# A SwiGLU stage rewritten as one list of block products, with its loads and operand preparation issued further ahead

## The chip, the cores and the metric

One core of a Trainium2 chip runs the whole program. The metric is device time in microseconds of one execution, taken several times; lower is better. A core has five engines that each run their own instruction queue in order: TensorE (PE, matrix products into PSUM), VectorE (DVE, elementwise work), ScalarE (ACT, copies with rounding and activation functions), GpSimd (POOL, some elementwise work, and here mostly a queue that issues DMAs) and SyncE (SP, a queue that issues DMAs). DMA transfers run beside them. An instruction that waits holds up everything behind it on its own engine.

## The reference

A decoder layer on x of 1024 tokens by 1024 channels in float32. First a token mixer in three groups of channels, then the feed-forward part, which is what the change is about:

```python
    h = rms_norm(x, g_ffn[l])
    x = x + (jax.nn.silu(h @ w_gate[l]) * (h @ w_up[l])) @ w_down[l]
return rms_norm(x, g_final)
```

`w_gate` and `w_up` are 1024 x 2816, `w_down` is 2816 x 1024. Below, "gate/up" is the pair of products with `w_gate` and `w_up`, and "down" is the product with `w_down`.

## The kernel before

Every float32 product is made of three matmuls (`mm3`, lines 322 to 324) on a high and a low part of each operand. The high part is a rounded copy made on ACT, the low part is the difference, made on DVE.

**Gate/up.** The 2816 columns are taken in 11 blocks of 256. For each block there are two "halves", gate (j = 0) and up (j = 1): 22 objects of the class `Half`, numbered k = 2p + j. A half is a 2 x 2 block product done with seven block products instead of eight (the Strassen-Winograd scheme), numbered 1 to 7. One product is 4 x 3 = 12 matmuls of 128 x 128 by 128 x 512, so a half is 84 matmuls. The right operands are the activations (B11, B21, B22, T1 in the two big tiles `bb`, and T2, T3, T4 computed once by `t_ops`). The left operands come from the weights:

- `Half.load` reads two weight tiles r1 and r2 through SP (line 868) and lets a DMA from POOL add one part of r2 onto another (`add`, line 874: a DMA with accumulation).
- `prep("A1")` makes the high and low parts of r1 (`ha` on ACT at line 853, `la` on DVE at line 854) for products 1 and 2.
- `prep("S1")`, `prep("S2")`, `prep("S3")`, `prep("A22")`, `prep("S4")` each make the high part (`S.copy`, line 879, on ACT) and the low part (line 880, on DVE) of one operand. After S1 an accumulating DMA turns the same place of r2 into S2's sum; after S2 two more make the sums of S4 and S3. So S1, S2 and then S3 and S4 are a chain with a DMA between its links.
- Products 1 and 2 use A1, product 5 uses S1, 6 uses S2, 7 uses S3, 4 uses A22 and 3 uses S4.

The parts lie in a pool `s5` of N5 = 9 slots; A1 takes two and every other operand one, so a half takes seven. The weight tiles lie in `crx`, four slots, which is two halves. Evacuation from PSUM combines the seven products into the tiles c1 and c2: line 917 (ACT) after product 1, 918 after 2, 933 and 934 after 6, 938 and 939 after 7, 943 after 4, 948 after 3, all on DVE. Products 5 and 4 share the PSUM tag `px` with two buffers, and the buffer of product 5 is read last at line 939. Then c1 and c2 are scaled by the row norm (line 950) and, for gate, go through Silu on ACT (lines 952 and 953). When both halves of a block are done, `lefts` (lines 1030 to 1039) multiplies them, forms the seven left operands of down and stores them in DRAM (`actd`).

`Rights` (lines 757 to 784) does the same for the right operands of down: it loads `w_down` (line 768), makes four sums (lines 774 to 777) and stores them (`td`, line 782), all its DMAs through SP. `middle(k)` puts `Rights` and `lefts` of the half before into the middle of half k.

**The order.** The source gives each instruction a place; a planner (`schedule_with_timeline_sim=True`) then simulates the program and fills each engine's queue. It takes an instruction as soon as its simulated inputs and a free slot are there, and the place in the source is its priority. The function `behind(x, y)` only says that y comes after x in its queue. So the order in a queue can differ from the order in the source, and on the chip a queue keeps the planned order even where the real times differ. In the source of before, a half's operands are prepared between its own products: S1 after product 1, S2 after product 5, S3 after 6, A22 after 7, S4 after 4 (for the first block S2 and S4 before product 3). The weights of half k + 1 are loaded at the start of half k. The first two halves are interleaved (1, 2, 5, 3 of both, then the rest), and so are the last two: 1, 2, 5 of both, then 6, 7, 4, 3 alternately.

**Down.** 77 operand tiles (i, p): product i in the order 1, 2, 5, 6, 3, 7, 4, and block p from 0 to 10. A tile has a left half from `actd` (line 1174) and a right half from `w_down` or `td` (line 1175), 256 KB each, both through SP. The first 27 go to 27 slots laid over memory of gate/up: the first eight over the big tile of B11 and T1, the next eleven over the T operands, the last eight over the big tile of B21 and B22. Each tile is split into parts by ACT (line 1116) and DVE (line 1117) and used in 12 matmuls. The tile (1, 10), the last of product 1, needs `actd` of the last block, which `lefts` of the last two halves stores through POOL. After it come four loads of the residual x1 (1 MB each, line 1177) and of `g_final` (line 1178) through POOL; evacuation of product 1 adds onto the first of them.

Of the kernel before, what the change touches and what calls it, by code (L numbers as in the profile page):

```python
# [3 lines left out]

# [1 line left out]

# [5 lines left out]
F32 = mybir.dt.float32  # L12
# [6 lines left out]
P = 128  # L19
D = 1024  # L20
NT = 1024
KD = D // P
DFF = 2816
NF = DFF // P
# [8 lines left out]
N4, N5, NSB, NWO = (int(v) for v in '11,9,4,6'.split(","))  # L33
# [11 lines left out]
def trunk(ctx: ExitStack, tc: tile.TileContext, A, O):  # L45
    nc = tc.nc
    V, S, GP, PE, SY = nc.vector, nc.scalar, nc.gpsimd, nc.tensor, nc.sync
    mult, add, sub = ALU.mult, ALU.add, ALU.subtract

    def en(key, i=0, default="0"):  # L50
        v = ENG.get(key, default)
        return GP if v[i % len(v)] == "1" else V

    def behind(first, *later):

        for i in later:
            tc.add_manual_dep(i.ins, first.ins.name, mybir.DependencyInfo(mybir.DependencyClass.NoSync, mybir.DependencyReason.DATA), reason="order")
# [8 lines left out]
    x1d = dram.tile([P, 8, 2, 512], F32, name="x1d")  # L66
# [278 lines left out]
    for k in range(KD):  # L345
# [4 lines left out]
        w = load_w(k, 0, 384, V, V if k == 0 else S)  # L350
# [25 lines left out]
    with tc.high_priority():  # L376
# [32 lines left out]
    e = V  # L409
# [347 lines left out]
    class Rights:  # L757
# [3 lines left out]
            o.p, h = divmod(k, 2)  # L761
            o.c, o.n = slice(h * 256, h * 256 + 256), f"{o.p}{h}"

        def load(o, first):
            o.r = [tr.tile([P, 2, 256], F32, tag=f"t{q}", name=f"t{q}_{o.n}") for q in range(2)]
            o.x = tr.tile([P, 256], F32, tag="x", name=f"tx_{o.n}")
            for q, r in enumerate(o.r):
                i = SY.dma_start(r, wd[o.p, q].rearrange("r (q c) -> r q c", q=2)[:, :, o.c])
                if first is not None:
                    behind(first, i)  # L770

# [4 lines left out]
            V.tensor_tensor(r1[:, 1], r1[:, 1], r0[:, 1], add)  # L776
            V.tensor_tensor(r1[:, 0], r1[:, 0], r1[:, 1], add)

        def store(o, first):
            r0, r1 = o.r  # L780
            for d, t in ((td[o.p, 2, :, o.c], o.x), (td[o.p, 3, :, o.c], r0[:, 1]), (td[o.p, 0:2, :, o.c].rearrange("q r c -> r q c"), r1)):
                i = SY.dma_start(d, t)
                if first is not None:
                    behind(first, i)

# [72 lines left out]
    class Half:  # L858


        def __init__(o, p, j):
            o.p, o.j, o.P, o.w = p, j, {}, {}
            o.n = f"{p}{j}"

        def load(o):
# [40 lines left out]
                mm3(pz, h[:, ks], l[:, ks], rh, rl, kt == 0, kt == 3)  # L906
            o.P[i] = pz

        def first(o):
            a = slice(0, 512)  # L910
            if o is not g0:
                o.prep("A1")
            o.prod(1, "A11", "B11")
            o.prep("S1")
            o.prod(2, "A12", "B21")
            o.c1, o.c2 = (cc.tile([P, NT], F32, tag="c", name=f"c{q}{o.n}") for q in range(2))
            S.copy(o.c2[:, a], o.P[1])
            o.last1 = V.tensor_tensor(o.c1[:, a], o.P[2], o.c2[:, a], add)
            o.prod(5, "S1", "T1")
            o.prep("S2")  # L920
            if o.p == 0:
                o.prep("S4")
                o.prod(3, "S4", "B22")

        def second(o):
            for _ in o.steps():
                pass

        def steps(o):

            a, b = slice(0, 512), slice(512, 1024)
            o.prod(6, "S2", "T2")
            V.tensor_tensor(o.c2[:, a], o.c2[:, a], o.P[6], sub)
            V.tensor_tensor(o.c1[:, b], o.c2[:, a], o.P[5], sub)
            o.prep("S3")
            yield
            o.prod(7, "S3", "T3")
            V.tensor_tensor(o.c2[:, a], o.P[7], o.c2[:, a], add)
            V.tensor_tensor(o.c2[:, b], o.c2[:, a], o.P[5], sub)  # L939
            o.prep("A22")  # L940
            yield
            o.prod(4, "A22", "T4")
            V.tensor_tensor(o.c2[:, a], o.c2[:, a], o.P[4], sub)
            if o.p:
                o.prep("S4")
                yield
                o.prod(3, "S4", "B22")
            o.last = V.tensor_tensor(o.c1[:, b], o.P[3], o.c1[:, b], add)
            for q, c in enumerate((o.c1, o.c2)):
                en('rs', 2 * o.j + q, '0101').tensor_tensor(c, c, rsf, mult)  # L950
            if o.j == 0:
                S.activation(o.c1, o.c1, AF.Silu)
                S.activation(o.c2, o.c2, AF.Silu, scale=-1.0)

    g0 = Half(0, 0)
# [47 lines left out]
    def t_ops():  # L1003

        for name in ("T2", "T3", "T4"):
            for kt in range(4):
                t2 = t2r[kt // 2][:, kt % 2]
                e = t_slot(f"{name}_{kt}")
                tt_[name, kt] = e
                eg = en(name, kt).tensor_tensor  # L1010
                w = t2
                if name == "T3":
                    hi, lo = b_op("B11", kt)
                    if kt % 2 == 0:
                        wt = ct.tile([P, NT], F32, tag="t", name=f"w{name}{kt}")
                    w = wt[:, (kt % 2) * 512:(kt % 2) * 512 + 512]
                    eg(w, t2, hi, sub)
                    eg(w, w, lo, sub)
                elif name == "T4":
                    hi, lo = b_op("B21", kt)  # L1020
                    eg(w, hi, w, sub)
                    eg(w, w, lo, add)
                S.copy(e[:, 0], w)
                en(name, kt).tensor_tensor(e[:, 1], w, e[:, 0], sub)

    def lefts(p, g, u):

        a, b = slice(0, 512), slice(512, 1024)
        c1, c2, d1, d2 = g.c1, g.c2, u.c1, u.c2
        V.tensor_tensor(c1, c1, d1, mult)  # L1030
        V.tensor_tensor(c2, c2, d2, mult)
        V.tensor_tensor(d1[:, b], c1[:, a], c1[:, b], add)
        V.tensor_tensor(c1[:, b], c1[:, b], c2[:, b], add)
        V.tensor_tensor(d1[:, a], c1[:, a], c1[:, b], add)
        V.tensor_tensor(d2[:, a], d1[:, a], c2[:, a], add)
        e = GP if p == NF // 2 - 1 else S
        for q, t in ((0, c1), (2, c2), (4, d1)):
            e.dma_start(actd[p, q:q + 2].rearrange("q r c -> r q c"), t.rearrange("r (q c) -> r q c", q=2))
        e.dma_start(actd[p, 6], d2[:, a])

    NH = NF
    H = [g0] + [Half(*divmod(k, 2)) for k in range(1, NH)]
    R = [Rights(k) for k in range(NH)]

    def middle(k):

        ld = H[k + 1].ld if k + 1 < NH else None
        if k:
            R[k - 1].sums(H[k - 1].last)
            R[k - 1].store(ld)  # L1050
        R[k].load(ld)
        if k > 1 and k % 2 == 0:
            lefts(k // 2 - 1, H[k - 2], H[k - 1])

    H[0].first()
    H[1].load()
    H[1].first()
    t_ops()
    ffn_rms()
    R[0].load(H[1].ld)  # L1060
    H[0].second()
    H[2].load()
    R[0].sums(H[0].last)
    R[0].store(H[2].ld)
    R[1].load(H[2].ld)
    H[1].second()
    for k in range(2, NH - 2):
        H[k + 1].load()
        H[k].first()
        middle(k)  # L1070
        H[k].second()
    g, u = H[NH - 2:]
    u.load()
    g.first()
    middle(NH - 2)
    u.first()
    R[NH - 2].sums(g.last1)
    R[NH - 2].store(u.ld)
    R[NH - 1].load(u.ld)
    for _ in zip_longest(g.steps(), u.steps()):  # L1080
        pass
    lefts(NF // 2 - 1, g, u)
    R[NH - 1].sums(g.last)
    R[NH - 1].store(None)
    psA.close()
    scC.close()
    sc4.close()
# [83 lines left out]
    for m, (i, p) in enumerate(todo):  # L1171
        if m >= len(SLOTS):
            early[i, p] = dr.tile([P, NT], F32, tag=f"r{SLOTS[m % len(SLOTS)]}", name=f"d{i}_{p}")
        SY.dma_start(early[i, p][:, a], actd[p, LEFT[i]])
        SY.dma_start(early[i, p][:, b], right(i, p))
    for i, h in ((0, 0), (0, 1), (1, 1), (1, 0)):
        GP.dma_start(cs[i, h], x1d[:, 4 * i:4 * i + 4, h])
    GP.dma_start(gfin, A["g_final"])

    def acc(c, x, op=add):  # L1180
        V.tensor_tensor(c, c, x, op)  # L1181
# [112 lines left out]
```

## Time and profile before

| | us |
|---|---|
| median of 3 runs (1040.85 to 1049.59) | 1043.83 |
| the profiled execution | 1045.06 |
| its span, first to last instruction | 1043.0 |
| PE busy in the span | 944.2 |
| DVE busy | 759.4 |
| ACT busy | 353.3 |
| POOL busy | 213.8 |

The busy time of PE is close to the span, so what can be gained lies in the places where PE waits or runs at a reduced clock. The span has these stretches: the token mixer up to about 340 us, gate/up from there to about 800 us, down to the end. The clock row of the profile's second part tells at what share of full speed PE was allowed to run in each slice.

### The profile page before, as it was taken

To read this page: it belongs to the slowest core of one execution; us is meant where nothing else is said; L and a number is where in the kernel's file an instruction comes from. 1 tells how busy PE (TensorE), PEld (TensorE's weight loads), DVE (VectorE), ACT (ScalarE), POOL (GpSimd) and SP (SyncE) were. 2 spreads that over 40 slices of the span, in tenths; PEclk is the share of its full clock that TensorE was granted. 3 is DMA by queue.
4 is the path that set the end of the run, shared out by engine and by line. 5 is a ranking of instruction groups with operands and counts; after the bars stand their busy time and mean duration, and the time that the engine had idled before them with its cause. 6 is when DMAs were issued, how large, how long until landed. Compare 5 with 4: busy or idle time off the path is not lost. (4 is left out here: it accounts for less than half of the span.)

```text
span 1043.0 us, 12545 instructions
## 1 busy us (share of the span) xinstructions
PE 944.2 (91%) x4280; PEld 780.9 (75%) x4280; DVE 759.4 (73%) x1275; ACT 353.3 (34%) x535; POOL 213.8 (20%) x234
## 2 busy tenths in 40 slices
PE   9988898687997999989997998998997959999996
PEld 7887697466886778867886886876885848888884
DVE  7999988964558988758767687676878436456776
ACT  7524232234334433222321322213222234343543
POOL 0346444412201511111111111111110200000032
PEclk9999899898999899998998999999999979999999
DMA  7234424337123368776767776777765999763012
GB/s 261 81 96 82 120 71 111 100 73 201 51 101 101 61 170 245 204 180 192 197 188 189 191 201 175 210 203 178 202 178 179 397 387 386 243 195 108 1 41 121
DMA packets 102016, 173.84 MB, mean 167 GB/s; under 512 B 13009, under 2 KB 46561, under 8 KB 101953
## 3 DMA queue, kind: packets, MB, share of 16 engines
q1 hardware_dynamic: 69344, 113.21, 33.4%
q0 software_dynamic: 14416, 29.63, 14.7%
q10 hardware_dynamic: 18192, 30.21, 9.0%
q8 instruction: 33, 0.54, 0.2%
q14 instruction: 31, 0.25, 0.1%
HBM read 110.00 MB, written 41.68 MB: 145 GB/s over the span
## 5 line engine op out<-in xcount | busy, mean ns | idle before, releaser
L1117 DVE TENSOR_TENSOR ol<-d,oh 128x1024 fp32r<-128x1024 f32 x77 | 95.9, 1258 | 87.7 <-PE q L324 52.4
L880 DVE TENSOR_TENSOR S<-r,S 128x512 fp32r<-128x512 f32 x88 | 62.0, 706 | 106.9 <-ACT S L879 106.8
L879 ACT CAST S<-r 128x512 fp32r<-128x512 f32 x88 | 54.1, 618 | 242.8 <-DMA r<-r 149.1
L322 PE MATMUL q<-oh 128*128 128x512 f32 x308 | 115.9, 399 | 15.1 <-ACT oh L1116 15.1
L874 POOL DMA_DIRECT2D r<-r x66 | 56.8, 861 | 348.2 <-DVE S L880 173.1
L323 PE MATMUL q<-ol,oh 128*128 128x512 f32 x308 | 121.5, 395 | 1.9 <-DVE ol L1117 1.9
L324 PE MATMUL q<-oh,ol 128*128 128x512 f32 x308 | 121.2, 394 | 0.0
L1116 ACT CAST oh<-d 128x1024 fp32r<-128x1024 f32 x77 | 80.7, 1053 | 119.1 <-PE q L324 70.5
L322 PE MATMUL p<-bb,S 128*128 128x512 f32 x176 | 73.3, 418 | 25.0 <-DVE c L939 24.4
L322 PEld LDWEIGHTS q<-oh 128*128 128x128 f32 x308 | 59.3, 193 | 28.5 <-ACT oh L1116 15.9
L324 PE MATMUL p<-bb,S 128*128 128x512 f32 x176 | 71.5, 407 | 0.0
L323 PE MATMUL p<-bb,S 128*128 128x512 f32 x176 | 71.3, 406 | 0.0
L322 PE MATMUL p<-bb,ha 128*128 128x512 f32 x176 | 69.8, 397 | 1.1 <-ACT ha L853 1.1
L324 PE MATMUL p<-bb,la 128*128 128x512 f32 x176 | 68.7, 393 | 1.6 <-DVE la L854 1.5
L322 PE MATMUL p<-T,S 128*128 128x512 f32 x176 | 69.1, 392 | 1.1 <-ACT S L879 0.6
L323 PEld LDWEIGHTS q<-ol,oh 128*128 128x128 f32 x308 | 58.9, 191 | 14.8 <-DVE ol L1117 2.3
L323 PE MATMUL p<-bb,ha 128*128 128x512 f32 x176 | 69.4, 394 | 0.0
L323 PE MATMUL p<-T,S 128*128 128x512 f32 x176 | 68.8, 391 | 0.0
L324 PE MATMUL p<-T,S 128*128 128x512 f32 x176 | 68.4, 389 | 0.0
L324 PEld LDWEIGHTS q<-oh,ol 128*128 128x128 f32 x308 | 58.8, 191 | 12.2
L322 PEld LDWEIGHTS p<-bb,S 128*128 128x128 f32 x176 | 35.2, 200 | 36.3 <-ACT ha L853 27.2
L323 PE MATMUL wo<-wo,yT 128*128 128x512 f32 x128 | 51.3, 402 | 7.7 <-DVE wo L601 7.7
(377 smaller groups left out, 2179.9 us busy)
## 6 DMA issues: line engine op xcount, KB each, us to landing
r<-in_w_gu SPq DMA_DIRECT2D x44, 512.0 KB, 4.0
d<-actd SPq DMA_DIRECT2D x77, 256.0 KB, 5.3
r<-r POOLq DMA_DIRECT2D x66, 256.0 KB, 4.4
actd<-c ACTq DMA_DIRECT2D x30, 512.0 KB, 4.6
t<-in_w_down SPq DMA_DIRECT2D x44, 256.0 KB, 3.6
d<-td SPq DMA_DIRECT2D x44, 256.0 KB, 5.1
d<-in_w_down SPq DMA_DIRECT2D x33, 256.0 KB, 5.4
r<-in_w_gu POOLq DMA_DIRECT2D x22, 256.0 KB, 4.8
```

What stands on the lines that cost most here:

```text
L322: PE.matmul(out, lh, rh, start=start, stop=False)
L323: PE.matmul(out, lh, rl, start=False, stop=False)
L324: return PE.matmul(out, ll, rh, start=False, stop=stop)
L874: GP.dma_start(dst, src, accum_op=add)
L879: S.copy(hi, src)
L880: V.tensor_tensor(lo, src, hi, sub)
L1116: S.copy(h, tv)
L1117: V.tensor_tensor(l, tv, h, sub)
```

## The change

The methods `first`, `second` and `steps` of `Half` become one method `step(i)`, which issues product i and its evacuation. The products of all halves are one list `seq`, in the same order as before. The operand preparations are a second list `preps` in the order of first use. `ahead()` is called after every product and issues every preparation whose slot (the one used nine places earlier in the list) has seen its last product in the source. When the six preparations of half k are issued, the load of half k + 2 is issued. `middle(k)` comes after product 5 (6 for the first two halves).

In the last two halves `Rights` uses the POOL queue for its loads and stores instead of SP. The sums of the last `Rights` are put behind the last evacuation of the last half instead of that of the half before it. The four loads of x1 and the load of `g_final` go through SP instead of POOL: the first behind the tile 11 of down, two behind tile 24, one behind tile 36, `g_final` after tile 40.

```diff
-        def first(o):
-            a = slice(0, 512)
-            if o is not g0:
-                o.prep("A1")
-            o.prod(1, "A11", "B11")
-            o.prep("S1")
-            o.prod(2, "A12", "B21")
...
-            o.prod(5, "S1", "T1")
-            o.prep("S2")
...
+        def step(o, i):
 
             a, b = slice(0, 512), slice(512, 1024)
...
+            o.prod(i, *{1: ("A11", "B11"), 2: ("A12", "B21"), 5: ("S1", "T1"), 6: ("S2", "T2"), 7: ("S3", "T3"), 4: ("A22", "T4"), 3: ("S4", "B22")}[i])
...
+            elif i == 2:
+                o.last = V.tensor_tensor(o.c1[:, a], o.P[2], o.c2[:, a], add)
...
-            for q, c in enumerate((o.c1, o.c2)):
-                en('rs', 2 * o.j + q, '0101').tensor_tensor(c, c, rsf, mult)
+            for c in (o.c1, o.c2):
+                V.tensor_tensor(c, c, rsf, mult)
...
+    E = NH - 2
+    seq = [(k, i) for k in (0, 1) for i in (1, 2, 5, 3)] + [(k, i) for k in (0, 1) for i in (6, 7, 4)]
+    seq += [(k, i) for k in range(2, E) for i in (1, 2, 5, 6, 7, 4, 3)]
+    seq += [(k, i) for k in (E, E + 1) for i in (1, 2, 5)] + [(k, i) for i in (6, 7, 4, 3) for k in (E, E + 1)]
...
+    def ahead():
+
+        nonlocal at, ld
+        while preps:
+            k, w = preps[0]
+            n = 2 if w == "A1" else 1
+            if any(q >= N5 and places[q - N5] not in done for q in range(at, at + n)):
+                return
+            preps.pop(0)
+            at += n
+            if (k, w) != (0, "A1"):
+                H[k].prep(w)
+            made[k] = made.get(k, 0) + 1
+            if made[k] == 6 and k + 2 < NH:
+                H[k + 2].load()
+                ld = H[k + 2].ld
 
     def middle(k):
 
-        ld = H[k + 1].ld if k + 1 < NH else None
+        q, first = (SY, ld) if k < E else (GP, None)
         if k:
             R[k - 1].sums(H[k - 1].last)
-            R[k - 1].store(ld)
-        R[k].load(ld)
+            R[k - 1].store(q, first)
+        R[k].load(q, first)
...
+    for k, i in seq:
+        H[k].step(i)
+        done.add((k, i))
+        ahead()
+        if i == (5 if k > 1 else 6):
+            middle(k)
...
-    R[NH - 1].sums(g.last)
-    R[NH - 1].store(None)
+    R[NH - 1].sums(H[E + 1].last)
+    R[NH - 1].store(GP, None)
...
-        SY.dma_start(early[i, p][:, b], right(i, p))
-    for i, h in ((0, 0), (0, 1), (1, 1), (1, 0)):
-        GP.dma_start(cs[i, h], x1d[:, 4 * i:4 * i + 4, h])
-    GP.dma_start(gfin, A["g_final"])
+        t = SY.dma_start(early[i, p][:, b], right(i, p))
+        for r, h in {11: ((0, 0),), 24: ((0, 1), (1, 1)), 36: ((1, 0),)}.get(m, ()):
+            behind(t, SY.dma_start(cs[r, h], x1d[:, 4 * r:4 * r + 4, h]))
+        if m == 40:
+            SY.dma_start(gfin, A["g_final"])
```

More of the change, by code (lines that the diff above doesn't have):

```diff
@@ L2 @@
 from contextlib import ExitStack
-from itertools import zip_longest
 import numpy as np
@@ L762, in __init__, with load @@
             o.c, o.n = slice(h * 256, h * 256 + 256), f"{o.p}{h}"
-        def load(o, first):
+        def load(o, e, first):
             o.r = [tr.tile([P, 2, 256], F32, tag=f"t{q}", name=f"t{q}_{o.n}") for q in range(2)]
@@ L767, in load @@
             for q, r in enumerate(o.r):
-                i = SY.dma_start(r, wd[o.p, q].rearrange("r (q c) -> r q c", q=2)[:, :, o.c])
+                i = e.dma_start(r, wd[o.p, q].rearrange("r (q c) -> r q c", q=2)[:, :, o.c])
                 if first is not None:
@@ L777, in sums, with store @@
             V.tensor_tensor(r1[:, 0], r1[:, 0], r1[:, 1], add)
-        def store(o, first):
+        def store(o, e, first):
             r0, r1 = o.r
             for d, t in ((td[o.p, 2, :, o.c], o.x), (td[o.p, 3, :, o.c], r0[:, 1]), (td[o.p, 0:2, :, o.c].rearrange("q r c -> r q c"), r1)):
-                i = SY.dma_start(d, t)
+                i = e.dma_start(d, t)
                 if first is not None:
@@ L861, in __init__ @@
         def __init__(o, p, j):
-            o.p, o.j, o.P, o.w = p, j, {}, {}
+            o.p, o.j, o.P, o.w, o.left = p, j, {}, {}, [1, 2, 3, 4, 5, 6, 7]
             o.n = f"{p}{j}"
@@ L907, in prod @@
             o.P[i] = pz
-        def first(o):
-            a = slice(0, 512)
-            if o is not g0:
-                o.prep("A1")
-            o.prod(1, "A11", "B11")
-            o.prep("S1")
-            o.prod(2, "A12", "B21")
-            o.c1, o.c2 = (cc.tile([P, NT], F32, tag="c", name=f"c{q}{o.n}") for q in range(2))
-            S.copy(o.c2[:, a], o.P[1])
-            o.last1 = V.tensor_tensor(o.c1[:, a], o.P[2], o.c2[:, a], add)
-            o.prod(5, "S1", "T1")
-            o.prep("S2")
-            if o.p == 0:
-                o.prep("S4")
-                o.prod(3, "S4", "B22")
@@ L925, in second @@
[L925 to L929, printed above, removed]
-            a, b = slice(0, 512), slice(512, 1024)
[L932 to L947, printed above, removed]
+        def step(o, i):
+            a, b = slice(0, 512), slice(512, 1024)
+            o.prod(i, *{1: ("A11", "B11"), 2: ("A12", "B21"), 5: ("S1", "T1"), 6: ("S2", "T2"), 7: ("S3", "T3"), 4: ("A22", "T4"), 3: ("S4", "B22")}[i])
+            if i == 1:
+                o.c1, o.c2 = (cc.tile([P, NT], F32, tag="c", name=f"c{q}{o.n}") for q in range(2))
+                S.copy(o.c2[:, a], o.P[1])
+            elif i == 2:
+                o.last = V.tensor_tensor(o.c1[:, a], o.P[2], o.c2[:, a], add)
+            elif i == 6:
+                V.tensor_tensor(o.c2[:, a], o.c2[:, a], o.P[6], sub)
+                V.tensor_tensor(o.c1[:, b], o.c2[:, a], o.P[5], sub)
+            elif i == 7:
+                V.tensor_tensor(o.c2[:, a], o.P[7], o.c2[:, a], add)
+                V.tensor_tensor(o.c2[:, b], o.c2[:, a], o.P[5], sub)
+            elif i == 4:
+                V.tensor_tensor(o.c2[:, a], o.c2[:, a], o.P[4], sub)
+            o.left.remove(i)
+            if o.left:
+                return
@@ L1043, in trunk @@
     R = [Rights(k) for k in range(NH)]
+    E = NH - 2
+    seq = [(k, i) for k in (0, 1) for i in (1, 2, 5, 3)] + [(k, i) for k in (0, 1) for i in (6, 7, 4)]
+    seq += [(k, i) for k in range(2, E) for i in (1, 2, 5, 6, 7, 4, 3)]
+    seq += [(k, i) for k in (E, E + 1) for i in (1, 2, 5)] + [(k, i) for i in (6, 7, 4, 3) for k in (E, E + 1)]
+    use = {1: "A1", 2: "A1", 5: "S1", 6: "S2", 7: "S3", 4: "A22", 3: "S4"}
+    preps = []
+    for k, i in seq:
+        for w in (("S2", "S4") if i == 3 else (use[i],)):
+            if (k, w) not in preps:
+                preps.append((k, w))
@@ new lines, in trunk @@
+    lastuse = {(k, use[i]): (k, i) for k, i in seq}
+    places = [lastuse[kw] for kw in preps for _ in range(2 if kw[1] == "A1" else 1)]
+    done, at, made = set(), 0, {0: 0, 1: 0}
+    ld = None
+    def ahead():
[4 more added lines that the diff above has]
+            if any(q >= N5 and places[q - N5] not in done for q in range(at, at + n)):
+                return
+            preps.pop(0)
[6 more added lines that the diff above has]
+                ld = H[k + 2].ld
@@ L1045, in middle @@
     def middle(k):
-        ld = H[k + 1].ld if k + 1 < NH else None
+        q, first = (SY, ld) if k < E else (GP, None)
         if k:
             R[k - 1].sums(H[k - 1].last)
-            R[k - 1].store(ld)
-        R[k].load(ld)
+            R[k - 1].store(q, first)
+        R[k].load(q, first)
         if k > 1 and k % 2 == 0:
             lefts(k // 2 - 1, H[k - 2], H[k - 1])
-    H[0].first()
     H[1].load()
[L1057 to L1082, printed above, removed]
-    R[NH - 1].sums(g.last)
@@ L1084, in trunk @@
-    R[NH - 1].store(None)
+    ld = H[1].ld
+    ahead()
+    for k, i in seq:
+        H[k].step(i)
+        done.add((k, i))
+        ahead()
+        if i == (5 if k > 1 else 6):
+            middle(k)
+        if (k, i) == (1, 3):
+            t_ops()
+            ffn_rms()
+    lefts(NF // 2 - 1, H[E], H[E + 1])
+    R[NH - 1].sums(H[E + 1].last)
+    R[NH - 1].store(GP, None)
     psA.close()
```

## The prediction

> **What bounds the kernel now.** I read the page's slices first, then busy time by stretches, then what PE waits for, then the queues around those waits in the timeline.
>
> ```profile
> span 1043.0 us, 12545 instructions
> PE   9988898687997999989997998998997959999996
> PEclk9999899898999899998998999999999979999999
> 400.00:450.00 50.00, 50.00 (x221) 41.08 (x221) 36.20 (x55) 12.58 (x19) 8.60 (x10) 1.00 0.83 227
> 450.00:790.00 340.00, 315.11 (x1346) 257.54 (x1345) 241.72 (x359) 87.44 (x131) 54.16 (x63) 0.96 0.71 189
> 800.40:814.70 14.30, 8.37 (x26) 6.21 (x26) 14.06 (x15) 7.18 (x7) 3.56 (x5) 0.76 1.02 350
> 814.70:836.40 21.70, 21.70 (x97) 17.80 (x95) 6.15 (x6) 4.21 (x4) 2.77 (x4) 1.00 1.03 394
> 836.40:854.00 17.60, 6.56 (x17) 5.05 (x17) 4.63 (x4) 6.13 (x8) 0.00 (x0) 0.61 1.04 387
> ```
>
> The columns behind the length are busy us and count for PE, weight load, DVE, ACT and POOL, then the granted clock, the DMA share and GB/s. From 400 to 450 us PE is never idle and issues 221 matmuls: 50/221 = 0.226 us each at full rate. Counted against that rate, three stretches lose time. From 450 to 790: 340/0.226 = 1503 possible, 1346 seen, 157 x 0.226 = 35.5 us. From 800.4 to 814.7: 63 possible, 26 seen, 8.4 us. From 836.4 to 854.0: 78 possible, 17 seen, 13.7 us. (A few records can be missing, which would make these smaller.) So 22.1 us go at the start of down and 35.5 in gate/up; 850 to 1000 loses nothing.
>
> Gate/up first. PE's idle time there has one cause in the list of waits, and the DVE queue shows what stands behind it (sums over 472 to 727, which is six pairs of halves, then the timeline):
>
> ```profile
> PE p L322 <- DVE c L939: 24.4, 7, 6.5
> 471.93:726.76 254.83, 236.90 (x1009) 193.62 (x1009) 179.46 (x265) 64.81 (x96) 41.27 (x48) 0.97 0.72 192
> L880 DVE TENSOR_TENSOR S<-r,S 128x512 fp32r<-128x512 f32 x48 | 33.0, 689 | 72.6 <-ACT S L879 72.5
> 448.97 0.39 PE L322 MATMUL p<-T,S 128*128 128x512 f32 x1
> 457.83 0.68 DVE L918 TENSOR_TENSOR c<-p,c 128x512 f32<-128x512 f32 x1
> 458.43 0.68 DVE L880 TENSOR_TENSOR S<-r,S 128x512 fp32r<-128x512 f32 x1
> 463.89 0.62 ACT L879 CAST S<-r 128x512 fp32r<-128x512 f32 x1 [5.63 <-DMA r<-r]
> 464.55 0.69 DVE L880 TENSOR_TENSOR S<-r,S 128x512 fp32r<-128x512 f32 x1 [5.43 <-ACT S L879]
> 465.15 0.68 DVE L933 TENSOR_TENSOR c<-c,p 128x512 f32<-128x512 f32 x1
> 468.69 0.69 DVE L880 TENSOR_TENSOR S<-r,S 128x512 fp32r<-128x512 f32 x1 [2.13 <-ACT S L879]
> 471.10 0.68 DVE L939 TENSOR_TENSOR c<-c,p 128x512 f32<-128x512 f32 x1
> 471.93 0.77 PE L322 MATMUL p<-bb,S 128*128 128x512 f32 x1 [6.48 <-DVE c L939]
> 487.43 0.69 DVE L880 TENSOR_TENSOR S<-r,S 128x512 fp32r<-128x512 f32 x1 [1.82 <-ACT S L879]
> 493.82 0.69 DVE L880 TENSOR_TENSOR S<-r,S 128x512 fp32r<-128x512 f32 x1 [2.32 <-ACT S L879]
> ```
>
> In six pairs DVE works 179.5 us and stands 72.6 us before the low parts of S: per pair 29.9 + 12.1 = 42.0, and a pair takes 254.8/6 = 42.5. PE needs 168 x 0.226 = 38.0. So **DVE's own queue sets the rate of gate/up**, its work plus the waits for the accumulating DMAs. Product 6 began at 448.97 and was over within 3 us, yet its evacuation (L933) ran at 465.15: it stood behind the next half's S2, which waited 5.43 us for its DMA. PE then lacks the PSUM buffer that L939 frees.
>
> **The start of down.** Two waits, and what SP and POOL did:
>
> ```profile
> 777.19 0.39 PE L324 MATMUL p<-bb,S 128*128 128x512 f32 x1
> 800.18 0.39 PE L324 MATMUL p<-bb,S 128*128 128x512 f32 x1
> 804.62 1.20 PE L322 MATMUL q<-oh 128*128 128x512 f32 x4 [4.06 <-ACT oh L1116]
> 847.63 3.78 PE L322 MATMUL q<-oh 128*128 128x512 f32 x8 [11.04 <-ACT oh L1116]
> 846.54 3.88 ACT L1116 CAST oh<-d 128x1024 fp32r<-128x1024 f32 x4 [20.55 <-DMA d<-actd]
> 797.70 1.76 SPq L782 DMA_DIRECT2D td<-t  x2
> 799.56 0.41 SPq L1174 DMA_DIRECT2D d<-actd  x1
> 841.08 1.00 SPq L1174 DMA_DIRECT2D d<-actd  x2
> 820.79 2.23 POOL L1177 DMA_DIRECT2D c<-x1d  x3 [6.72 <-issue]
> c<-x1d POOLq DMA_DIRECT2D x4, 1024.0 KB, 11.5
> ```
>
> SP issues the first tile of down at 799.56, right behind the last store of `Rights`, though the last product that reads the first eight slots' memory (5 of the last half) was issued by 777.2. And ACT's eleventh split, tile (1, 10), waits until 846.5 for an `actd` half that SP issued only at 841.08, behind some 19 tiles that the planner put ahead of it, while the four x1 loads (4 x 1.05 = 4.2 MB, 10.6 us at the 394 GB/s seen there) shared the engines.
>
> **The change part by part.** The sum is made against the profiled execution's 1045.06 us (2.1 over its span).
>
> *Flat sequence, operands half ahead: 0.* It removes and adds no matmul, split or DMA; it gives preparations an earlier place in the source. But the queue of before already has them there: S1 of the next half (458.43) stands directly behind L918 of the present one (457.83), S2 before L933, though the source has them after all its evacuations. L918 follows product 2, and product 2 is what frees A1's slots, which S1 and S2 of the next half take nine places on. So the nine slots, not the place in the source, limit how early they come, and N5 stays 9. What is left is priority where two are ready at once, such as S1 against the work of `lefts`. Bounds: the two halves of the pair above differ, one waiting 5.43 + 2.13 = 7.6, the other 1.82 + 2.32 = 4.1. If both came to wait like the second, a pair would take 29.9 + 8.2 = 38.1, PE's own rate, and all 35.5 us go; if both like the first, 3.4 more in each of eight pairs, +27. I take 0, since the order is set by the same slots and the same DMA.
>
> *Weights two halves ahead: 0.* `crx` has four slots, two halves. A load can start only when the last split of the half two earlier has read its slot, as before. `Rights` on SP is now behind that later load; its place stays after it, as both were already.
>
> *Start of the stage: +1.* Two preparations come ahead of the T operands and the row norm; 2 x 0.69 of DVE is 1.4 if uncovered, 0 if covered, -1.4 if an operand is what is late.
>
> *`Rights` of the last two halves through POOL: +3.* 13 DMA issues (5 + 5 + 3) leave SP; five (x1, `g_final`) leave POOL.
>
> ```profile
> L874 POOL DMA_DIRECT2D r<-r x66 | 56.8, 861 | 348.2 <-DVE S L880 173.1
> 803.69 0.77 POOL L1038 DMA_DIRECT2D actd<-c  x1 [32.28 <-DVE c L1031]
> 785.15 0.42 DVE L774 TENSOR_TENSOR tx<-t,t 128x256 f32<-128x256 f32 x1 [5.15 <-DMA t<-in_w_down]
> t<-in_w_down SPq DMA_DIRECT2D x44, 256.0 KB, 3.6
> r<-in_w_gu POOLq DMA_DIRECT2D x22, 256.0 KB, 4.8
> actd<-c POOLq DMA_DIRECT2D x3, 512.0 KB, 7.7
> ```
>
> At 0.86 us each the issues cost POOL 11 us of the 32.28 in which it had nothing to do before 803.69. The price is latency: at 785.15 DVE already stands 5.15 us before these sums, with evacuations behind them. A store and a load lie ahead of them; by 4.8 against 3.6 they come 2.4 us later, by 7.7 (POOL's stores while down's tiles load, as they now will) 8 us later. If the planner moves the sums behind the evacuations, 0; and the last `Rights`, now behind the last evacuation, takes its four sums (4 x 0.42 = 1.7) out of its way. I take 3, near the 4.8 row, and keep -1.7 and 8. The Trainium skill, in "DMA: Bandwidth & Descriptors", section "Latency and other measured facts", speaks against this edit: it gives a first byte after about 1 us through GpSimd against about 0.6 through the hardware path. By that, an estimate, two links would cost 0.8 and the sum would be 2 us lower; 4.8 against 3.6 is a wider gap, and here it decides.
>
> *SP free for down: -6.* Nothing of `Rights` stands before down's tiles. The first eight (4.2 MB, 10.6 us at 394 GB/s) can go from 777.4 and are there by about 790, before PE ends gate/up at 800.4. What stays is the split of the first tile behind DVE's last evacuations: I leave 2.4 of the 8.4 us. Bounds 0 (all stays, where DVE is late) and 8.4.
>
> *x1 loads spread: -12.* The late `actd` half now has at most 26 tiles (13.6 MB) and one x1 load (1.05) ahead of it, with 3.4 MB of stores and `Rights` beside: 18 MB, 46 us at 394, from 777.4 to 823; landing as before (846.54 - 841.08 = 5.5) gives 829, the split 830. PE needs it after 10 tiles x 12 x 0.226 = 27 us from 803, also 830. I leave 1.7 of the 13.7. Bounds: 13.7 and 0. The first x1 load must be there when product 1 ends, at 833; it stands after 12 tiles (6.3 MB, 16 us), so about 30 us ahead of that.
>
> The clock adds to such waits: after 11.04 us idle PE is still at a reduced rate for part of the time to 854.0, which makes 13.7 of 11.0. "TensorE: Matmul & The Clock Gate" of the Trainium skill, Part 1, says half rate until about 3.4 us of sustained work; by that the loss would be 11.0 + 1.7 = 12.7 and the sum, an estimate, 1 us higher. The row stands.
>
> Sum: 0 + 0 + 1 + 3 - 6 - 12 = -14, so 1031.1 for a run like the profiled one. That one lies 1.2 over the median, so against 1043.83 it is **1030 us**.
>
> **The rivals.**
>
> *A: the waits of DVE go too.*
>
> ```profile
> L1031 DVE TENSOR_TENSOR c<-c,c 128x1024 f32<-128x1024 f32 x6 | 7.4, 1226 | 0.2
> L1035 DVE TENSOR_TENSOR c<-c,c 128x512 f32<-128x512 f32 x6 | 4.2, 692 | 0.2
> ```
>
> The new priorities put the work of `lefts` (per pair two of 1.2 us and four of 0.69, some 5 us of DVE) between S1 and S2 instead of nothing. For it: the second half of the pair, with such work between, waits only 4.1. Against it: in the other half nothing else is ready there. All of it gives 1030 - 35 = 995, half of it 1012.
>
> *B: slower.* The splits come ahead of still more evacuations, because preparations now win against them, and both halves wait like the first: +27, so 1057. It decides from 3.1 us more per pair (25 in eight). For it: L933 behind S2 above. Against it: S2 and S3 can't be ready before their DMAs, whatever their priority.
>
> *C: the start of down stays late.* The `actd` half is behind the x1 load on one queue, and that load waits for memory that gate/up's last tiles hold, as 820.79 shows with 6.72 us before the three loads. SP stands there; only the first wait goes: 1043.83 + 4 - 6 = 1042.
>
> **How the numbers follow.** The forecast has 0.55, A 0.22, B 0.08, C 0.15. A measurement of this kernel tells about 1% (10 us) from no change. The forecast's own range moves two terms to their bounds: 1023 (both gains whole, POOL 0) to 1041 (POOL 8, half of the x1 gain). Below 1033.4 lie some 0.38 of its 0.55 and all of A: faster 0.60. The rest of it and C are within 1%: 0.32; B 0.08. The range 1006 to 1045 leaves out the deeper half of A and B, 0.19.
>
> **What would show it.** Per pair in the middle of gate/up: still about 42 us, DVE's waits before L880 about 12. First tile of down issued near 778; PE's wait at 804 under 3 us; no wait over 3 us at tile (1, 10). `t` sums of the last two blocks 2 to 3 us later. If a pair takes 38 to 40, A is right and the slots were not the limit; if over 45, B. If SP's first tile is again near 799, the SP step is wrong; if an x1 load stands on SP before tile (1, 10) and that comes after 830, C is.

## The result, and the profile after

The changed kernel took 1032.42 us, the median of 7 runs (1026.06 to 1035.52), against 1043.83 for 7 runs of before: ratio 0.988, 95% interval 0.985 to 0.992. The forecast was 1030 us, with a range of 1006 to 1045. The profiled execution took 1032.42 us as well, 12.6 less than that of before, and its span is 12.4 us shorter.

First the head of the page with PE's row of slices and the granted clock, then five stretches of the trace. The stretches have the times and the columns used for before: length, busy us and count for PE, weight load, DVE, ACT and POOL, then clock, DMA share and GB/s.

```profile
span 1030.6 us, 12532 instructions
PE   8988798697999799998997997999898799999996
PEclk9999899798999899999999999999999899999999
```

```profile
450.00:790.00 340.00, 317.19 (x1364) 260.25 (x1362) 238.91 (x356) 88.47 (x132) 58.63 (x70) 0.97 0.74 198
800.40:814.70 14.30, 9.10 (x31) 7.04 (x30) 13.36 (x18) 6.83 (x7) 3.74 (x6) 0.76 1.00 355
814.70:836.40 21.70, 21.70 (x98) 17.95 (x97) 10.97 (x11) 8.19 (x8) 0.83 (x2) 1.00 1.01 379
836.40:854.00 17.60, 17.60 (x80) 14.56 (x79) 10.51 (x11) 8.54 (x11) 0.00 (x0) 1.00 1.04 380
```

The last row has changed most. From 836.4 to 854.0 PE issued 17 matmuls before and issues 80 now: the hole of 13.7 us at tile (1, 10) is filled. The start of down, in the second row, went from 26 matmuls to 31, about 1 us. Gate/up, in the first row, went from 1346 to 1364, which is 4 us gained from 450 on. Up to 450 us the changed kernel has issued 10 matmuls fewer (1959 since the start of the span, against 1969), so at 790 it is some 2 us ahead. It loses that and 2.9 us more by the end of gate/up, as is seen below.

Gate/up in detail: what PE waits for from 400 to 840 us, six pairs of halves, the group of S low parts on DVE in them, and the timeline at the place that the prediction showed of before.

```profile
PE p L321 <- DVE c L922: 26.8, 7, 5.7
PE q L322 <- DVE ol L1115: 5.2, 1, 5.2
```

```profile
472.28:725.36 253.08, 234.92 (x1008) 192.67 (x1009) 179.85 (x266) 64.89 (x96) 41.26 (x48) 0.97 0.72 194
```

```profile
L879 DVE TENSOR_TENSOR S<-r,S 128x512 fp32r<-128x512 f32 x49 | 33.7, 688 | 70.4 <-ACT S L878 70.4
```

```profile
458.64 0.68 DVE L916 TENSOR_TENSOR c<-p,c 128x512 f32<-128x512 f32 x1
459.25 0.68 DVE L879 TENSOR_TENSOR S<-r,S 128x512 fp32r<-128x512 f32 x1
...
465.66 0.69 DVE L879 TENSOR_TENSOR S<-r,S 128x512 fp32r<-128x512 f32 x1 [5.74 <-ACT S L878]
466.27 0.68 DVE L918 TENSOR_TENSOR c<-c,p 128x512 f32<-128x512 f32 x1
...
472.28 0.47 PE L321 MATMUL p<-bb,S 128*128 128x512 f32 x1 [4.65 <-DVE c L922]
```

It is the same picture with other line numbers (L916 was L918, L879 was L880, L918 was L933, L922 was L939). S1's low part follows the sum of product 2. S2's low part stands next, waits 5.74 us for its DMA (5.43 before), and the evacuation of product 6 runs only after it. A pair takes 253.1/6 = 42.2 us (42.5 before), and DVE stands 70.4/6 = 11.7 us in it (12.1 before). The flat sequence changed the source and not this queue.

The start of down, from the timeline of SP, DVE and PE:

```profile
776.29 0.33 SPq L1172 DMA_DIRECT2D d<-actd  x1
788.18 0.43 DVE L773 TENSOR_TENSOR tx<-t,t 128x256 f32<-128x256 f32 x1 [4.79 <-DMA t<-in_w_down]
794.01 0.79 PE L321 MATMUL p<-T,A 128*128 128x512 f32 x1 [3.75 <-DVE c L922]
803.08 0.39 PE L323 MATMUL p<-bb,S 128*128 128x512 f32 x1
803.30 1.07 PE L321 MATMUL q<-oh 128*128 128x512 f32 x4
808.30 1.21 DVE L1115 TENSOR_TENSOR ol<-d,oh 128x1024 fp32r<-128x1024 f32 x1
809.57 0.80 PE L322 MATMUL q<-ol,oh 128*128 128x512 f32 x1 [5.20 <-DVE ol L1115]
815.25 4.88 SPq L1172 DMA_DIRECT2D d<-actd  x2
831.75 1.70 SPq L1175 DMA_DIRECT2D c<-x1d  x3
```

SP issues the first tile at 776.29 instead of 799.56, and PE no longer waits for the tile's high part. After four matmuls it stops 5.20 us for the low part instead, which DVE makes only at 808.30, behind the last evacuations and `lefts`. The sums of `t` at 788.18 stand 4.79 us for POOL's load, three us later than before, PE waits 3.75 at 794.01 behind them, and gate/up ends at 803.08 instead of 800.18. The late `actd` half goes out by 820 instead of 841.08, and the x1 loads, three of them at 831.75, come after it. The account by matmuls at 0.226 us: gate/up ends 2.9 us later, and the last three rows above have 5, 1 and 63 matmuls more than before, 69 x 0.226 = 15.6. That leaves 12.7, and the spans differ by 12.4.

### The profile page after: what moved, and what is told of

The parts are those of the page before. It is cut to its first block, busy times and chain, and to the rows that moved or that the text cites. A ratio compares the mean times of both kernels' runs of the same rounds, so it can differ in the third digit from the quotient of the medians.

```text
span 1030.6 us, 12532 instructions
## 1 busy us (share of the span) xinstructions
PE 940.9 (91%) x4280; PEld 779.9 (76%) x4280; DVE 759.0 (74%) x1275; ACT 352.7 (34%) x535; POOL 218.4 (21%) x242
## 3 DMA queue, kind: packets, MB, share of 16 engines
q1 hardware_dynamic: 68832, 115.30, 34.2%
## 5 line engine op out<-in xcount | busy, mean ns | idle before, releaser
L879 DVE TENSOR_TENSOR S<-r,S 128x512 fp32r<-128x512 f32 x88 | 61.9, 705 | 94.7 <-ACT S L878 94.7
L321 PEld LDWEIGHTS q<-oh 128*128 128x128 f32 x308 | 58.3, 189 | 12.1
```

Source lines behind the costliest of these rows:

```text
L321: PE.matmul(out, lh, rh, start=start, stop=False)
L879: V.tensor_tensor(lo, src, hi, sub)
```

## The experiments

All times are medians; each ratio is to runs of before on the same chip.

**The change taken apart.** Five kernels ask which edit removed the wait of 11 us and what the others cost. `x1_only` is before with the x1 loads of the change, and nothing else:

```diff
-    for i, h in ((0, 0), (0, 1), (1, 1), (1, 0)):
-        GP.dma_start(cs[i, h], x1d[:, 4 * i:4 * i + 4, h])
+        for r, h in {11: ((0, 0),), 24: ((0, 1), (1, 1)), 36: ((1, 0),)}.get(m, ()):
+            behind(t, SY.dma_start(cs[r, h], x1d[:, 4 * r:4 * r + 4, h]))
```

> The kernel before, with only the loads of x1 and g_final moved to SP (behind tiles 11, 24, 36 and 40). Theory P (the prediction's terms): the late actd half of tile (1, 10) is issued some 10 us earlier, near 831, because 4.2 MB no longer share the engines before it; PE's wait of 11 us shrinks to under 2; ratio 0.988 to 0.990, SP's first tile still near 799.5. Rival Q (SP being held by Rights is the whole cause): the wait stays over 8 us and the ratio is 0.997 or more.

`rights_only` is before with the last two halves' `Rights` on POOL and the last sums behind the last half:

```diff
-    R[NH - 2].store(u.ld)
-    R[NH - 1].load(u.ld)
+    R[NH - 2].store(GP, None)
+    R[NH - 1].load(GP, None)
...
-    R[NH - 1].sums(g.last)
-    R[NH - 1].store(None)
+    R[NH - 1].sums(u.last)
+    R[NH - 1].store(GP, None)
```

> The kernel before, with only Rights of the last two halves moved to POOL; x1 stays on POOL too. Theory P: SP issues its first tile near 777; the first wait of down shrinks by up to 6 us, gate/up ends 3 us later, and the 11 us wait stays for the larger part: ratio 0.995 to 0.999. Rival Q: because SP starts 22 us earlier, the actd half is issued before the x1 loads have begun, the 11 us wait goes without any change to x1, and the ratio is 0.988 to 0.991.

`x1_and_rights` has both diffs, which is the changed kernel without the flat sequence:

> The kernel before with both moves, without the flat sequence. If the flat sequence is worth nothing: the changed kernel's ratio, 0.986 to 0.990. If the flat sequence carries some of the gain: 0.993 or more.

`flat_only` is the changed kernel with those two parts undone:

```diff
-        q, first = (SY, ld) if k < E else (GP, None)
+        q, first = SY, ld
...
-    R[NH - 1].sums(H[E + 1].last)
-    R[NH - 1].store(GP, None)
+    R[NH - 1].sums(H[E].last)
+    R[NH - 1].store(SY, None)
...
-        for r, h in {11: ((0, 0),), 24: ((0, 1), (1, 1)), 36: ((1, 0),)}.get(m, ()):
-            behind(t, SY.dma_start(cs[r, h], x1d[:, 4 * r:4 * r + 4, h]))
+    for i, h in ((0, 0), (0, 1), (1, 1), (1, 0)):
+        GP.dma_start(cs[i, h], x1d[:, 4 * i:4 * i + 4, h])
```

> The changed kernel with Rights back on SP (and its last sums behind the evacuation they had before) and x1 back on POOL: only the flat sequence is left. Theory P: ratio 0.997 to 1.003, DVE's waits before the low parts of S within 5 us of the 93 us in 450 to 790 of the kernel before, PE's two waits at the start of down as before. Rival A: DVE's waits fall under 75 us and the ratio is under 0.985.

And `flat_x1` is `flat_only` with the x1 loads on SP again, so that only the `Rights` differ from the changed kernel:

> The changed kernel with Rights of the last two halves back on SP (its last sums behind the evacuation they had before): flat sequence and x1 on SP. If moving Rights to POOL costs more than it gives once x1 is on SP: faster than the changed kernel, ratio to before 0.981 to 0.986, gate/up ends 3 to 5 us sooner than with Rights on POOL and PE has no wait over 3.5 us at the start of down. If the move to POOL is needed: 0.988 or more, with a wait of several us at tile (1, 10).

| kernel | us | ratio to before, 95% interval | longest waits of PE after 790 us |
|---|---|---|---|
| x1_only | 1030.44 | 0.985 (0.982 to 0.988) | 3.09, 0.88 |
| rights_only | 1034.86 | 0.989 (0.986 to 0.992) | 4.36, 5.21 |
| x1_and_rights | 1032.84 | 0.989 (0.985 to 0.992) | 2.98, 5.21 |
| flat_only | 1041.69 | 0.997 (0.995 to 0.998) | 1.90, 2.27, 9.66 |
| flat_x1 | 1030.54 | 0.986 (0.984 to 0.989) | 4.73, 0.33 |

The wait at tile (1, 10) is there with the flat sequence alone (9.66 us) and gone with either of the other two parts alone. How each does it shows in the queues: the `actd` half on SP in `x1_only`, with ACT's split behind it, and in `rights_only` the half and the x1 loads, still on POOL.

```profile
825.70 1.00 SPq L1174 DMA_DIRECT2D d<-actd  x2
831.15 4.85 ACT L1116 CAST oh<-d 128x1024 fp32r<-128x1024 f32 x5 [11.06 <-DMA d<-actd]
```

```profile
816.98 5.37 SPq L1174 DMA_DIRECT2D d<-actd  x2
825.52 2.23 POOL L1177 DMA_DIRECT2D c<-x1d  x3 [4.97 <-issue]
```

In `x1_only` the half is issued at 825.70 instead of 841.08. SP's first tile is 3.2 us earlier in this execution (796.36), and no x1 load shares the DMA engines ahead of the half (10.6 us at the rate of before). ACT still waits 11.06 us for it, but is through before PE needs the tile. In `rights_only` SP starts 22 us earlier and has the half out by 822.4, ahead of most of x1. Each moves it by 15 us or more where 11 were missing, so the second of them finds nothing left. What it then adds is its price: with x1 moved, moving the `Rights` too goes from 1030.44 to 1032.84, and in the flat kernels, from two sets of runs, from 1030.54 to 1032.42. The intervals overlap, so 2 us are not shown by the times. In the traces gate/up ends later with the `Rights` on POOL in each of three pairs: 805.14 against 800.18 (`rights_only`, before), 802.49 against 798.06 (`x1_and_rights`, `x1_only`), 803.08 against 800.89 (changed, `flat_x1`). That is 2.2 to 5.0 us, where before and `x1_only`, which have the same gate/up, differ by 2.1: the sign is the same three times, the size is open. Down gains nothing for it once x1 is moved. From the end of gate/up to the end of the span it takes 227.6 us in `x1_only`, 227.7 in `x1_and_rights` and 242.9 in before.

Theory P gave `flat_only` and, with a larger gain than it forecast, `x1_only`; `rights_only` went by rival Q. `flat_x1` fits neither of its two theories: it is no slower than the changed kernel and has no wait at tile (1, 10), but its gate/up ends 2.2 us sooner and not 3 to 5, and PE waits 4.73 us at the start of down, where SP issues its first tile only at 800.28.

The flat sequence alone gives 0.997, four us. In the traces nearly all of that lies in down (239.1 us in place of 242.9), in the waits that the other two parts remove too. With the x1 loads beside it, it gives nothing (0.986 against 0.985), and with all parts nothing (0.988 against 0.989). DVE's waits before S parts from 450 to 790 are 88.0 us in `flat_only` and 89.0 in `flat_x1`, against 93.1 in before.

**What sets the rate of gate/up.** The prediction laid 35.5 us to DVE's queue and its waits for accumulating DMAs. `no_accumulate` is `flat_x1` without these three DMAs; it leaves out the additions of weights that S2, S3 and S4 are made of, and so computes another product.

```diff
                 o.split(r2[:, a], "S1")
-                o.add(r2[:, a], r1[:, a])
             elif wn == "S2":
                 o.split(r2[:, a], "S2")
-                o.add(r2[:, a], r1[:, b])
-                o.add(r1[:, a], A["w_gu"][2 * o.p + 1, :, o.j, a])
```

> As flat_x1, leaving out the three accumulating DMAs behind S1 and S2, so that S2, S3 and S4 are made from the plain weights and wait for no sum. DVE does the same number of instructions. Theory: with no DMA between the links, DVE's waits before the low parts of S go to under 20 us in 450 to 790, a pair takes 38 to 39 us, 25 to 35 us less in all than flat_x1. Rival: PE still waits for evacuations and a pair takes over 41 us, so DVE's work or something else is the limit.

It took 987.76 us (2 runs), ratio 0.945 (0.941 to 0.950): 43 us less than `flat_x1`, more than was forecast. Its stretch from 450 to 740 us, and the S group on DVE from 450 to 790:

```profile
450.00:740.00 290.00, 290.00 (x1281) 240.19 (x1281) 232.30 (x340) 84.55 (x120) 12.01 (x14) 1.00 0.56 173
```

```profile
L879 DVE TENSOR_TENSOR S<-r,S 128x512 fp32r<-128x512 f32 x61 | 41.3, 687 | 9.1 <-ACT S L878 8.9
```

PE is never idle and keeps the full clock; 290/1281 = 0.226 us per matmul is the rate of before at its best. So with these DMAs gone, nothing else in the stage holds gate/up back. But the kernel also moves less data, which this run does not tell from the waits, and some 11 of the 43 us lie ahead of 450 us (2003 matmuls issued by then, 1952 in `flat_x1`). It says what the DMAs cost, not that it can be had.

**Waiting later instead of not at all.** If S2's low part did not stand in DVE's queue ahead of evacuations that are ready, the DMA could run under them. `late_s2_s3` is `flat_x1` with S2 of a half held back behind the evacuation of product 4 of the half before it and S3 behind that of product 3, in the source and by `behind` on the low part (`o.ev[i]` is the last DVE instruction of product i):

```diff
+            if (wn in LATE) and 3 <= k <= E:
+                behind(H[k - 1].ev[LATE[wn]], i)
...
+    LATE = {'S2': 4, 'S3': 3}
...
+            if w in LATE and 3 <= k <= E and (k - 1, LATE[w]) not in done:
+                return
             preps.pop(0)
```

> As flat_x1, with two orders added on DVE's queue: the low part of S2 of half k stands behind the evacuation of product 4 of half k - 1, and that of S3 behind the evacuation of its product 3 (before: S2 directly behind S1 or after the first evacuations). No work is added or removed. Theory (DVE's own queue, its work plus its waits for the accumulating DMAs, sets the rate of gate/up): DVE's waits before the low parts of S in 450 to 790 fall from some 90 us to under 45, PE's waits on the evacuation after product 7 nearly vanish, a pair of halves takes 38 to 39.5 us in place of 42.4, and the time falls by a further 20 to 35 us against flat_x1: ratio to before 0.950 to 0.965. Rival (the waits are only a sign: PE's clock, the DMA rate or the preparation chain set the rate): the operands S2 and S3 come late instead, PE waits on the S parts, and the time is within 8 us of flat_x1 or above it.

It missed: 1030.72 us, 0.986 (0.983 to 0.989), nothing gained on `flat_x1`. Both groups of low parts on DVE from 450 to 790, then the timeline of one place:

```profile
L879 DVE TENSOR_TENSOR S<-r,S 128x512 fp32r<-128x512 f32 x66 | 45.0, 682 | 3.2 <-ACT S L878 3.2
...
L879 DVE TENSOR_TENSOR A<-r,A 128x512 fp32r<-128x512 f32 x17 | 11.7, 691 | 92.2 <-ACT A L878 92.2
```

```profile
470.57 0.62 ACT L878 CAST S<-r 128x512 fp32r<-128x512 f32 x1 [3.28 <-DMA r<-in_w_gu]
471.10 0.62 ACT L878 CAST A<-r 128x512 fp32r<-128x512 f32 x1
471.75 0.69 DVE L879 TENSOR_TENSOR A<-r,A 128x512 fp32r<-128x512 f32 x1 [8.30 <-ACT A L878]
472.36 0.68 DVE L927 TENSOR_TENSOR c<-c,p 128x512 f32<-128x512 f32 x1
```

The S parts wait 3.2 us instead of 89.0, and the A22 parts 92.2 instead of 0. A22 needs no DMA, so the planner gives its low part an early place on DVE, ahead of the evacuation of product 4 (L927). But on ACT its cast stands behind S3's, and that one waits for the accumulating DMA. The same DMA now reaches DVE through ACT's queue. PE's waits moved too, as the rival had it: from the evacuation after product 7 (23.8 us in `flat_x1`) to the low parts of S.

```profile
PE p L323 <- DVE S L879: 24.8, 22, 2.1
```

Two kernels test that A22's place is the cause, each `late_s2_s3` with one more edit. `late_s2_a22_s3` holds A22 back as well; `early_a22_late_s2_s3` prepares it right behind S1, ahead of anything that waits:

```diff
-    LATE = {'S2': 4, 'S3': 3}
+    LATE = {'S2': 4, 'A22': 3, 'S3': 3}
```

```diff
+    for k in range(2, E):
+        preps.remove((k, "A22"))
+        preps.insert(preps.index((k, "S1")) + 1, (k, "A22"))
```

> As late_s2_s3 (1030.72 us), but the A22 part's low half is held back behind the evacuation of product 3 of the half before as well, so that on DVE no A22 subtraction stands ahead of the evacuations while ScalarE's A22 cast waits behind the S3 cast and its DMA. Theory C (DVE's queue gave the lost time back only because the wait moved from the S parts to the A22 part, 92.2 us from 450 to 790): the waits of DVE for ACT's S and A22 casts together fall under 40 us in that stretch and the time to 995 to 1015 us. Rival D (ScalarE's own queue, where the S3 cast waits for its DMA, now sets the pace: la, or the copy of product 1, comes late): DVE's waits move to L853 or to the sum of product 2, and the time stays within 8 us of 1030.7.

> As late_s2_s3 (1030.72 us), but A22, which no DMA changes, is prepared right behind S1 on ScalarE and DVE, ahead of S2, instead of behind S3. Theory C: no A22 subtraction waits, DVE's waits for S and A22 casts from 450 to 790 fall under 30 us and the time to 990 to 1010 us, a little under the other kernel, since A22 fills ScalarE's queue while S1's DMA is under way. Rival D: the wait moves once more, to S4 or to la behind the S3 cast in ScalarE's queue, and the time stays within 8 us of 1030.7. Rival E: A22 takes a slot of the nine of s5 earlier and holds it longer, so that PE waits for S2 or S3 parts: more than 25 us of PE waits on S low parts, time 1025 to 1040.

They took 994.64 us, 0.954 (0.952 to 0.957), and 994.10 us, 0.955 (0.953 to 0.957). Theory C holds in both: either way of taking A22 out from behind S3 gives back what `late_s2_s3` lost. DVE's waits before S parts from 450 to 760 us are 22.0 and 19.7 us, before A22 parts none, and the times lie at the lower end of what was forecast, the first 0.4 us under it. Of `late_s2_a22_s3`, two stretches, the S and A22 groups on DVE from 450 to 760, and the place of S2 in the timeline:

```profile
400.00:450.00 50.00, 50.00 (x222) 41.30 (x221) 37.96 (x59) 11.08 (x17) 9.25 (x11) 1.00 0.89 248
450.00:760.00 310.00, 310.00 (x1369) 256.77 (x1369) 242.56 (x364) 86.72 (x132) 54.26 (x63) 1.00 0.79 212
```

```profile
L879 DVE TENSOR_TENSOR S<-r,S 128x512 fp32r<-128x512 f32 x66 | 45.2, 685 | 22.0 <-ACT S L878 22.0
...
L879 DVE TENSOR_TENSOR A<-r,A 128x512 fp32r<-128x512 f32 x17 | 11.6, 684 | 0.0
```

```profile
459.20 0.68 DVE L921 TENSOR_TENSOR c<-c,p 128x512 f32<-128x512 f32 x1
...
462.21 0.69 DVE L927 TENSOR_TENSOR c<-c,p 128x512 f32<-128x512 f32 x1
464.91 0.62 ACT L878 CAST S<-r 128x512 fp32r<-128x512 f32 x1 [7.53 <-DMA r<-r]
465.56 0.69 DVE L879 TENSOR_TENSOR S<-r,S 128x512 fp32r<-128x512 f32 x1 [2.66 <-ACT S L878]
...
766.02 0.39 PE L323 MATMUL p<-bb,S 128*128 128x512 f32 x1
```

S2's low part runs at 465.56, when it ran at 464.55 in before: it has not become earlier. But the evacuations of products 6, 7 and 4 now lie ahead of it, from 459.20 on, under the DMA. What is left of its wait costs nothing, since PE is busy through all 360 us; gate/up ends at 766.0. Before ended it at 800.2, and with the 13.7 us at tile (1, 10) that makes 47.9, of a measured 1041.72 - 994.64 = 47.1. Against `flat_x1`, from which it differs only in these orders, it is 35.9 us faster, and gate/up ends 34.9 us sooner.

Last, the same hold on the changed kernel with its `Rights` on POOL:

> The changed kernel (1032.42 us), Rights of the last two halves on POOL and all, with the S2, A22 and S3 parts held back as in late_s2_a22_s3 (994.64 us). Theory C (the waits behind S and A22 casts set the pace of gate/up, whatever the Rights do): 992 to 1000 us, PE's 222 matmuls in each 50 us from 400 to 750. Theory R (the Rights on POOL keep their price of 2 to 5 us, because the sums of t, behind the last evacuations in DVE's queue, wait for POOL's loads): the time is 2 to 5 us over 994.6, 996.5 to 1000, with a PE wait of over 2 us in the last 15 us of gate/up. Rival: at the faster pace gate/up meets the moved loads in its last pair and loses more, over 1000 us.

It took 996.05 us, 0.953 (0.950 to 0.957). PE issues 222 or 223 matmuls in every 50 us from 450 to 750. There is no wait at all in the last 15 us of gate/up, only the 5.20 us for the first low part of down, so theory R's place is not there any more; and a difference of 1.4 us in the times, on two chips, is not told from none. The version that beats both kernels is any of these three; by the ratios none is better than the others.

## Why the prediction was right, point by point

**What bounds the kernel: right.** DVE's queue sets the rate of gate/up through its waits for accumulating DMAs: `no_accumulate` takes the DMAs away, `late_s2_a22_s3` and `early_a22_late_s2_s3` only move the ready work ahead of the waits, and PE keeps its full rate in all three. Estimated were 35.5 us lost; 34.2 were had back at its end (800.2 to 766.0).

**Flat sequence, 0: right.** A pair went from 42.5 to 42.2 us, the waits before S stayed, and with and without it the other parts give the same time. That the order of S1 and S2 in the queue is the same is seen; that the nine slots are what fixes it was argued, and no kernel with more slots was tried. What does fix the rate is narrower than the prediction's wording: it said that S2 and S3 can't be ready before their DMAs, whatever their priority. That is so, but the work behind them can be moved ahead, and rival A's 995 us is just what that gives. Rival A was sound as a price and not an effect of this change: it moves preparations forward in the source, and the gain lay in putting them further back in the queue.

**Weights two halves ahead, 0, and start of the stage, +1: nothing seen against them.** Neither was tried alone; `flat_only` holds both and is not slower. Up to 450 us the three kernels with the flat sequence have issued 1952 to 1959 matmuls, before and the three others 1961 to 1973, some 2 us for the start. From 450 to 790 they issue 1357 to 1363 against 1344 to 1354 and have it back, which no term of the prediction had.

**`Rights` through POOL, +3: right in sign, put low.** Gate/up ended 2.9 us later, by the late load named in the prediction (the `t` sums three us later, then a wait of PE). But the changed kernel was some 2 us ahead at 790, so the end of gate/up lost about 5. That is near the 4.8 us that the two links cost more on POOL (last section), where 2.4 were reckoned from the medians; DVE reached the chain 2 us earlier, so its sums are only three us late. The sums of the last block, forecast 2 to 3 us later, came 9 us later (805.03 against 795.77), since they now stand behind the last evacuations. The price holds for this pace of gate/up: where DVE no longer waits for S, the cost isn't seen.

**SP free for down, -6: mis-sized.** The first tile came at 776.29, as forecast near 778, and the high part's wait went. But the remainder behind DVE's last evacuations was put at 2.4 us, and measured 5.20, the wait for the first `ol`; the stretch gained 1 us. The step that failed is the leave of 2.4, for DVE's queue was not followed to the first `ol`. The prediction's own sign for the term, PE's wait at 804 under 3 us, did not come. In before the first `ol` already stood late, and PE waited for it after the high part:

```profile
806.42 1.22 DVE L1117 TENSOR_TENSOR ol<-d,oh 128x1024 fp32r<-128x1024 f32 x1
807.70 0.80 PE L323 MATMUL q<-ol,oh 128*128 128x512 f32 x1 [1.87 <-DVE ol L1117]
```

So 4.06 + 1.87 = 5.9 us became 5.20. `x1_only`, where SP issues its first tile only at 796.36, 1.7 us before gate/up ends, waits 3.09 + 0.88 = 4.0 us there: with the x1 loads moved, this term is worth nothing. In the changed kernel the `ol` comes 1.9 us later still, as gate/up ends 2.9 us later. DVE's queue just ahead of it:

```profile
805.03 0.41 DVE L773 TENSOR_TENSOR tx<-t,t 128x256 f32<-128x256 f32 x1
805.36 1.22 DVE L930 TENSOR_TENSOR c<-c,rsf 128x1024 f32<-128x1024 f32 x1
806.50 0.42 DVE L774 TENSOR_TENSOR t<-t 128x256 f32<-128x256 f32 x1
806.83 1.22 DVE L1010 TENSOR_TENSOR c<-c,c 128x1024 f32<-128x1024 f32 x1
807.97 0.41 DVE L775 TENSOR_TENSOR t<-t,t 128x256 f32<-128x256 f32 x1
```

Three of the last four sums of `t`, which the change puts behind the last evacuations, stand there with 1.2 us; the prediction had them only leave the evacuations' way.

**x1 loads spread, -12: right in size, wrong as a term of its own.** All 13.7 us went. But the prediction reckoned the term with both edits in place, SP free from 777.4 and one x1 load ahead, and each alone removes the wait. The gain is there without the move to POOL, and with it the x1 loads add nothing that the times show (1034.86 against 1032.84). The x1 loads did not spread as the source has them either: three were issued together at 831.75 and none behind tile 11, so the reckoning of one load and 18 MB ahead of the late half was not what happened. No evacuation waited for them.

The sum, -14 against -12.4 in the trace, is in part luck. Gate/up was put at +4 and came to +2.9, where a loss of about 5 us at its end met 2 us gained before it. Down was put at -18 and came to -15.3 (242.9 to 227.6), where SP's term gave about 1 of 6 and the x1 term nearly 14 of 12. Rivals B and C are out: from 450 us on no pair takes over 45 us, and SP was not late.

## What to carry to other kernels

An engine's queue is served in order, so an instruction that waits for a DMA costs all the ready work behind it: put that work ahead of it, and let the DMA run under it, before trying to start the DMA earlier. When such a wait is moved, follow every queue that the waiting value passes through, for it comes back at the next instruction that is innocent itself (here A22, behind S3 on ACT). And when two edits attack one wait, the gain is that of the wait and not the sum; price each as if the other had been done.

## What was not expected of the hardware

A chain that went to POOL's queue lost more here than the medians of issue to landing tell. The chain in the last pair of gate/up is a last sum of `t`, its store, the load into the same tile, the next sums. Before had it on SP, the changed kernel on POOL:

```profile
777.71 0.54 SPq L782 DMA_DIRECT2D td<-t  x1
781.30 0.55 SPq L768 DMA_DIRECT2D t<-in_w_down  x1
```

```profile
775.91 0.73 POOL L781 DMA_DIRECT2D td<-t  x1
781.74 0.71 POOL L767 DMA_DIRECT2D t<-in_w_down  x1 [5.10 <-DMA td<-t]
```

From store to load it is 3.6 us on SP and 5.8 on POOL. From load to the first sum (785.15 before, 788.18 now) it is 3.9 and 6.4. Two links cost 2.2 + 2.6 = 4.8 us. The prediction weighed the Trainium skill here, "DMA: Bandwidth & Descriptors", section "Latency and other measured facts", whose first bytes (about 1 us through GpSimd, about 0.6 through the hardware path) make 0.8 of two links, an estimate. The trace does not agree in size, though in sign. How much of it is POOL's queue stays open, for down's tiles now load at the same time. The same store and load ran ahead of SP's first tile in `changed_and_late` (740.73 to 745.56, the tile at 745.69) and took 4.8 us; beside the tiles they took 5.2 in `x1_and_rights` and 7.4 in `rights_only`. On SP they took 2.4 us in `flat_only`, 4.0 in `flat_x1` and 4.8 in `x1_only`. So a loss by the queue alone is not shown, and the tiles are likely to make much of it.

The second is the clock. With PE never idle from 450 to 760 us in `late_s2_a22_s3` the granted clock is 1.00, where before has 0.96 from 450 to 790. In before a wait costs more than it lasts. Behind the 6.48 us that end at 471.93 PE's timeline goes on like this:

```profile
474.20 0.63 PE L324 MATMUL p<-bb,S 128*128 128x512 f32 x1
474.62 0.63 PE L322 MATMUL p<-bb,S 128*128 128x512 f32 x1
```

The matmuls start 0.43 us apart up to 478.04, for 6.1 us, and 0.23 us apart after that. Behind the 11.04 us of tile (1, 10) they are 0.43 us apart for 5.7 us, from 847.63 to 853.35. Each time some 3 us go that are no wait, which is how 11.04 us of waiting lose 13.7. Most of the difference between the 24.9 us in which PE is idle from 450 to 790 (340 - 315.11) and the 35.5 that are lost there is of this kind.
